# A two-layer attention trunk: half-row score products widened to 128 rows, latent scores in three split products, two residual column groups kept in DRAM

## The chip, the core and the metric

The kernel runs on one core of one Trainium2 chip. The metric is the device time of one execution in microseconds, the median of several runs; lower is better. The core's engines are named as in the profile: PE (TensorE, matrix products), PEld (its weight loads), DVE (VectorE), ACT (ScalarE), POOL (GpSimd) and SP (SyncE, which here issues every DMA).

## What is computed

The input x is 512 frames of 2048 channels, float32. Each of two layers does the following.

```
proj = rmsnorm(x) @ w_in           # 2048 -> dq, dk, dv (1024 each), cq 512, ckv 256, kr 64, gate 2048
# (A) differential attention, 8 heads, two softmax maps of width 64 per head
s = q @ k.T * scale + bias[:, m];  p = softmax(mask(s1)) - lam * softmax(mask(s2));  o_a = rmsnorm(p @ v)
# (B) latent attention, 8 heads: q and k/v come from the normalized latents cq and ckv
s = (qn @ kn.T + qr @ kr.T) * scale    # 128 plain channels per head and 64 rotary ones
o_b = softmax(mask(s)) @ v
x = x + (concat(o_a, o_b) * silu(gate)) @ w_out
```

A frame reads its own chunk of 64 frames and all earlier ones, so a block of 128 queries reads 128, 256, 384 or 512 keys. A last RMSNorm closes the trunk.

## The kernel before

**Split products.** A float32 operand is written as a high part (rounded to `fp32r`) and a low part (the rest). One product is then three products: high by high, high by low, low by high. `mm3` issues such a trio; nearly all of PE's work is trios of line 249 over projection weights. Products of plain float32 operands stand in the trace as two records each (`sc<-qkm`, line 523: 64 in the program, 128 in the trace).

**Weights.** Weights stream through a ring of units (2 or 4 blocks of 128 rows, 1024 columns in all). SP loads a unit to one of two `raw` buffers, ACT makes the high part (`whi`, line 195), DVE the low part (`wlo`, line 196), into four buffers each; when a unit is split, the load of the unit after the next one is issued (`pump`, `emit_dma`). The split runs up to two units ahead of PE. One unit is some 24 products of 512 columns.

**Order.** The program's order is written out by hand. A stage is a list of projection pieces for PE; `mix` spreads attention steps of the stage before between them. In a differential stage `i` the pieces project gates, values and queries/keys of two heads, and the steps are those of the two heads of stage `i-1`: `diff_scores` (step a), transposes of the probabilities (b), the product with v (c). In the latent part, stages `j` project two heads each (`mla_proj`) and a quarter of the output projection (`OD`, `j`), with the steps of `j-1` between them.

**Scores.** For 64-wide heads one product holds both parts of q: rows `half(m)` hold q's high part and the other 64 rows its low part, and k's high part stands in both halves. That gives high by high and low by high in one product over 128 rows (line 492). High by low is a second product that uses the 64 rows of `half(m)` alone (line 493):

```
nc.tensor.matmul(dst, lhsT=q[:, m], rhs=khi, start=first, stop=False)
nc.tensor.matmul(dst, lhsT=q[half(m), m], rhs=klo[half(m)], start=False, stop=True)
```

`diff_scores` does this for two maps (four products); `mla_scores` does a plain float32 product of the 128 unrotated channels (line 523) and then this pair for the rotary ones. There are 64 score steps of each kind in the program: 16 heads (8 per layer) by four widths.

**Buffers.** `big` has 16 pages of 8 KB per partition, which the residual `xs` (four column groups of 512), normalized activations, q/k pairs, gates and latents share. `evac_acc(c)` adds the first half of the output projection to `xs[c]`, `evac_om(c)` the second half, once all latent heads are done. `xs[c]` is loaded by `load_xc(c)` and stays in its page until then.

Of the kernel before, what the change touches and what calls it, by code (L numbers as in the profile page):

```python
# [14 lines left out]
ALU = mybir.AluOpType  # L15
# [39 lines left out]
def tile_hybrid_trunk(ctx, tc, x, norm_g, w_in, diff_lambda, diff_subln_g, mla_q_norm_g,  # L55
# [19 lines left out]
    bip = pool("bias", 2)  # L75
    tp = pool("tmp", 4)
    op = pool("o", 2)
    stp = pool("st", 16)
    keep = pool("keep", 4)
    krp = pool("kr", 1)  # L80
    klp = pool("kl", 3)
    pj = pool("pj", 4, bass.MemoryType.PSUM)
    at = pool("at", 4, bass.MemoryType.PSUM)
    dr = pool("dr", 1, bass.MemoryType.DRAM)
# [232 lines left out]
    with tc.manual_schedule():  # L317
# [12 lines left out]
        for q in range(4):  # L330
            load_x(x, 0, q)

        gsrc = const.tile([46, P], F32, name="gsrc")
        sp.dma_start(out=gsrc[0:32], in_=norm_g.rearrange("l (k p) -> (l k) p", p=P))
        sp.dma_start(out=gsrc[32:40], in_=mla_q_norm_g.rearrange("l (k p) -> (l k) p", p=P))
        sp.dma_start(out=gsrc[40:44], in_=mla_kv_norm_g.rearrange("l (k p) -> (l k) p", p=P))
# [5 lines left out]
        cosT = const.tile([P, NSB, ROPE], F32, name="cosT")  # L342
        sinT = const.tile([P, NSB, ROPE // 2], F32, name="sinT")
        dlam = B([P, DEPTH, 2, 2, DH], F32, "dlam")
        relb = const.tile([BUCKETS, MAPS], F32, name="relb")
        oneh = big.tile([BUCKETS, NVEC], F32, tag="B", name="oneh")
        def load_small():
            sp.dma_start(out=relb, in_=rel_bias)
            sp.dma_start(out=oneh, in_=onehot)
# [128 lines left out]
        def half(m):  # L478
            return slice(m * DH, (m + 1) * DH)
# [10 lines left out]
        def mm_stack(dst, q, khi, klo, m, first):  # L490

            nc.tensor.matmul(dst, lhsT=q[:, m], rhs=khi, start=first, stop=False)  # L492
            nc.tensor.matmul(dst, lhsT=q[half(m), m], rhs=klo[half(m)], start=False, stop=True)  # L493

        def diff_scores(l, hd, qb, bt, st_):
            w = (qb + 1) * P
            mx, sm = stat("mx"), stat("sum")
            s = []
            for m in range(2):
                bk = bank("sc")  # L500
                mm_stack(bk[:, :w], hd["qk"][:, 0, :, qb * P:(qb + 1) * P], hd["qk"][:, 1, m, :w], hd["kl"][:, :w], m, True)
                sm_t = T("s", smp, "sm")
                nc.vector.tensor_tensor_reduce(  # L503
                    out=sm_t[:, :w], in0=bk[:, :w], in1=bt[:, m, 512 - w:512], op0=ALU.add, op1=ALU.max,
                    scale=1.0, scalar=LOW, accum_out=mx[:, m:m + 1])
                s.append(sm_t)
            nc.vector.tensor_scalar(out=mx[:, 2:4], in0=mx[:, 0:2], scalar1=-1.0, scalar2=None, op0=ALU.mult)  # L507
            for m in range(2):
                nc.scalar.activation(s[m][:, :w], s[m][:, :w], AF.Exp, bias=mx[:, 2 + m:3 + m], accum_out=sm[:, m:m + 1])  # L509
            nc.vector.reciprocal(sm[:, 2:4], sm[:, 0:2])  # L510
            nc.vector.scalar_tensor_tensor(out=sm[:, 4:5], in0=sm[:, 3:4], scalar=neglam[:, l:l + 1], in1=sm[:, 0:1],
                                           op0=ALU.mult, op1=ALU.mult)
            nc.vector.scalar_tensor_tensor(out=s[0][:, :w], in0=s[1][:, :w], scalar=sm[:, 4:5], in1=s[0][:, :w],
                                           op0=ALU.mult, op1=ALU.add)
            st_["p"], st_["rc"] = s[0], sm[:, 2:3]

        def mla_scores(qk, par, j, rope, qb, st_):
            w = (qb + 1) * P
            scale = QH ** -0.5
            mx, sm = stat("mx"), stat("sum")  # L520
            bk = bank("sc")
            q = slice(qb * P, (qb + 1) * P)
            nc.tensor.matmul(bk[:, :w], lhsT=qk[:, par, q], rhs=qk[:, 2 + par, :w], start=True, stop=False)  # L523
            mm_stack(bk[:, :w], rope["q", j // 2][:, j % 2, :, q], rope["k"][:, 0, :w], rope["k"][:, 1, :w], par, False)
            nc.vector.memset(bk[0:CHUNK, w - CHUNK:w], NEG)
            nc.vector.tensor_reduce(out=mx[:, 0:1], in_=bk[:, :w], op=ALU.max, axis=AX.X)
            nc.vector.tensor_scalar(out=mx[:, 1:2], in0=mx[:, 0:1], scalar1=-scale, scalar2=None, op0=ALU.mult)  # L527
            s = T("s", smp, "sm")
            nc.scalar.activation(s[:, :w], bk[:, :w], AF.Exp, bias=mx[:, 1:2], scale=scale, accum_out=sm[:, 0:1])  # L529
            nc.vector.reciprocal(sm[:, 1:2], sm[:, 0:1])  # L530
            nc.vector.tensor_scalar(out=s[:, :w], in0=s[:, :w], scalar1=sm[:, 1:2], scalar2=None, op0=ALU.mult)
            st_["p"] = s
# [65 lines left out]
        def mla_items(l, j, qk, v, gate, rope):  # L598
            slots = []
            for hp in range(2):  # L600
                h = 2 * j + hp
                o_ = {}
                for qb in range(NSB):
                    st_ = {}

                    def a(hp=hp, qb=qb, st_=st_):
                        mla_scores(qk["t"], hp, j, rope, qb, st_)
                        if hp == 1 and qb == NSB - 1:
                            qk.pop("t")
                            if j % 2:  # L610
                                rope.pop(("q", j // 2))

                    def b(qb=qb, st_=st_):
                        transpose_p(qb, st_)

                    def c(hp=hp, qb=qb, o_=o_, st_=st_):
                        if qb == 0:
                            o_["bk"] = bank("oT")
                        for kb in range(qb + 1):
                            nc.tensor.matmul(o_["bk"][:, qb * P:(qb + 1) * P], lhsT=v["t"][:, kb, hp * P:(hp + 1) * P],  # L620
                                             rhs=st_["pt"][:, kb * P:(kb + 1) * P], start=kb == 0, stop=kb == qb)

                    slot = [a, b, c]
                    if qb == NSB - 1:
                        def d(h=h, o_=o_):
                            y = gate(h)
                            nc.vector.tensor_tensor(y, o_.pop("bk"), y, op=ALU.mult)

                        slot.append(d)
                    slots.append(slot)  # L630
            return pipeline(slots, MLAG)
# [5 lines left out]


        x1 = dr.tile([S, D], F32, name="x1")
        boundary = []  # L640
        for l in range(DEPTH):
            g = plan[l]
# [87 lines left out]
            for i in range(4):  # L730
                qk, v = {}, {}

                def evac_qk(b, bk, qk=qk):
                    if b < 2:
                        qk[b] = {"qk": B([P, 2, 2, S], F32R, "qk")}
                        split_stack(bk, qk[b]["qk"][:, 0], DH ** -0.5)
                        return
                    hd = qk[b - 2]
                    hd["kl"] = klp.tile([P, S], F32R, tag="kl", name="kl")
                    k = hd["qk"][:, 1]  # L740
                    for m in range(2):
                        acopy(k[half(m), m], bk[half(m)])
                    for m in range(2):
                        acopy(k[half(1 - m), m], bk[half(m)])
                        nc.vector.tensor_tensor(hd["kl"][half(m)], bk[half(m)], k[half(m), m].bitcast(F32), op=ALU.subtract)

                def evac_v(b, bk, v=v):
                    if "t" not in v:
                        v["t"] = vp.tile([P, NSB, 256], F32, tag="v", name="v")
                    (nc.vector.tensor_copy if b % 2 else acopy)(v["t"][:, b, :], bk[:, :256])  # L750

                pieces = []
                if i:
                    pieces += group(g["G", i - 1], 2, mm_T(ah), evac_gate(2 * i - 2))
                pieces += group(g["V", i], NSB, mm_S(ah, 256), evac_v, cost=2)
                pieces += group(g["QK", i], 4, mm_T(ah), evac_qk)
                mix(pieces, pend, MIX_DIFF)
                pend = diff_items(l, i, qk, v, gate_y)
# [22 lines left out]
            def load_xc(c, src=x if l == 0 else x1):  # L781
                for sb in range(NSB):
                    load_x(src, sb, c)

            load_xc(0)

            def act_y(y):
# [2 lines left out]
            def evac_acc(c):  # L790
                def evac(b, bk):
                    a = xs[c][:, b, :]
                    nc.vector.tensor_tensor(a, bk, a, op=ALU.add)
                return evac


# [97 lines left out]
            mix(group(g["QR"], NSB, mm_S(act_cq, 512), evac_qr), [])  # L894

            def mla_proj(j, qk, v):
                def evac_qn(b, bk):
                    if "t" not in qk:
                        qk["t"] = B([P, 4, S], F32, "qkm")
                    (nc.vector.tensor_copy if b % 2 else acopy)(qk["t"][:, b, :], bk)  # L900

                def mm_kv(bk, b, hi, lo, k, kb, first, last):
                    c = slice(b * 256, b * 256 + NOPE)
                    mm3(bk, (hi[:, k, c], lo[:, k, c]), act_kv(kb), True, first, last)

                def evac_kn(b, bk):
                    (nc.vector.tensor_copy if b % 2 else acopy)(qk["t"][:, 2 + b, :], bk)

                pieces = group(g["QN", j], 2, mm_T(act_cq), evac_qn)
                (u, _, _), = g["KV", j]  # L910
# [36 lines left out]
            for j in range(1, 4):  # L947
                pieces = mla_proj(j, *qkv[j]) + out_pieces(("OD", j), yd, evac_acc(j))
                if j == 3:
                    load_xc(3)  # L950
                    mix(pieces[:16], pend, MIX_MLA[2])
                    tail = pieces[16:]
                elif j == 2:
                    mix(pieces[:-8], pend, MIX_MLA[1])
                    load_xc(2)
# [114 lines left out]
```

## Time and profile before

| | |
|---|---|
| median of 3 runs | 1834.45 us (1833.92 to 1834.63) |
| profiled execution | 1835.62 us, span 1833.8 us |
| PE, PEld busy | 1804.4 us (98%), 1492.3 us (81%) |
| DVE, ACT, POOL busy | 952.9 us (52%), 710.1 us (39%), 32.2 us (2%) |
| DMA | 179.34 MB, 98 GB/s over the span |
| mean granted clock of TensorE | 0.997 |

The span is from the first to the last instruction of the profiled execution; its own time, 1835.62 us, also has what lies around it. PE's busy time counts a product until its modelled end, and products overlap in the pipeline: how long a product holds the engine is read from one start to the next.

### The profile page before, as it was taken

How to read it: one execution, taken by the hardware profiler on the slowest of the kernel's cores; microseconds unless marked ns; L12 is line 12 of the kernel's file. 1: busy time of each engine (PE TensorE's matmuls, PEld its weight loads, DVE VectorE, ACT ScalarE, POOL GpSimd, SP SyncE). 2: the span in 40 equal slices, each digit the busy share in tenths (PEclk: the TensorE clock that was granted, in tenths of full speed). 3: DMA queues.
4: the chain of work that ended last, by engine and by line, in shares of the span. 5: the costliest groups of instructions: out<-in, count | busy, mean ns of one | idle time of the engine just before them, and what ended most of it. 6: DMA issues, size and time to landing. Idle time of an engine off the chain costs nothing.

```text
span 1833.8 us, 23481 instructions
## 1 busy us (share of the span) xinstructions
PE 1804.4 (98%) x9245; PEld 1492.3 (81%) x9245; DVE 952.9 (52%) x1753; ACT 710.1 (39%) x1424; POOL 32.2 (2%) x53
## 2 busy tenths in 40 slices
PE   6999999999999999999999999999999999999997
PEld 4888888887878987878879887888887798878786
DVE  5426445453646774454362353644545667645554
ACT  5324444443443442333352343444443344433333
POOL 1000000000000000000000000000000000000000
PEclk9999999999999999999999999999999999999999
DMA  5543232232322431313333232323223224213223
GB/s 173 173 144 98 72 101 81 71 114 70 115 81 78 118 104 58 115 58 103 127 105 102 71 114 71 114 71 102 81 70 115 80 81 149 70 58 113 71 92 126
DMA packets 142330, 179.34 MB, mean 98 GB/s; under 512 B 16942, under 2 KB 94812, under 8 KB 142092
## 3 DMA queue, kind: packets, MB, share of 16 engines
q1 hardware_dynamic: 142220, 177.85, 31.7%
q8 instruction: 72, 1.18, 0.3%
q14 instruction: 38, 0.31, 0.1%
HBM read 169.39 MB, written 13.67 MB: 100 GB/s over the span
## 4 chain that ended last, share of the span: by engine, by line
PE 97%; ACT 1%; DVE 1%; issue 0%; DMA 0%; POOL 0%; SPq 0%; ACTq 0%; POOLq 0%; DVEq 0%
PE pj L249 81%; PE sc L493 4%; PE sc L492 2%; PE pT L309 2%; PE sc L523 2%; PE oT L620 2%; PE ov L573 2%; PE nT L309 1%; PE oT L309 0%; ACT xn L99 0%; PE cT L309 0%; ACT whi L195 0%; DMA xs<-in_x 0%; DVE nt L457 0%; POOL rs L314 0%
## 5 line engine op out<-in xcount | busy, mean ns | idle before, releaser
L196 DVE TENSOR_TENSOR wlo<-raw,whi 128x1024 fp32r<-128x1024 f32 (+1 forms) x272 | 327.7, 1211 | 323.9 <-ACT whi L195 316.5
L249 PE MATMUL pj<-hThi,whi 128*128 128x512 f32 x1024 | 413.6, 404 | 0.0
L249 PE MATMUL pj<-hThi,wlo 128*128 128x512 f32 x1024 | 400.0, 391 | 0.0
L249 PE MATMUL pj<-hTlo,whi 128*128 128x512 f32 x1024 | 399.5, 390 | 0.0
L195 ACT ACTIVATE whi<-raw 128x1024 fp32r<-128x1024 f32 (+1 forms) x272 | 282.6, 1047 | 180.6 <-PE pj L249 106.3
L249 PE MATMUL pj<-whi,yhl 128*128 128x512 f32 x1024 | 326.8, 400 | 0.0
L249 PE MATMUL pj<-whi,hThi 128*128 128x256 f32 (+2 forms) x768 | 243.1, 317 | 2.1 <-ACT hThi L99 2.1
L249 PE MATMUL pj<-whi,hTlo 128*128 128x256 f32 (+2 forms) x768 | 236.2, 308 | 0.0
L249 PE MATMUL pj<-wlo,hThi 128*128 128x256 f32 (+2 forms) x768 | 236.0, 307 | 0.0
L249 PEld LDWEIGHTS pj<-hThi,whi 128*128 128x128 f32 x1024 | 192.5, 188 | 43.3 <-issue 4.3
L249 PEld LDWEIGHTS pj<-hThi,wlo 128*128 128x128 f32 x1024 | 192.2, 188 | 41.4
L249 PEld LDWEIGHTS pj<-hTlo,whi 128*128 128x128 f32 x1024 | 192.8, 188 | 35.1
L249 PEld LDWEIGHTS pj<-whi,yhl 128*128 128x128 f32 x1024 | 184.3, 188 | 38.6 <-issue 3.5
L249 PE MATMUL pj<-wlo,yhl 128*128 128x512 f32 x512 | 200.5, 392 | 0.0
L509 ACT ACTIVATE s<-s,mx 128x128 f32<-128x128 f32 (+3 forms) x128 | 71.1, 557 | 294.0 <-DVE mx L507 294.0
L249 PEld LDWEIGHTS pj<-whi,hThi 128*128 128x128 f32 x768 | 147.2, 192 | 10.5 <-ACT hThi L99 2.5
L249 PEld LDWEIGHTS pj<-whi,hTlo 128*128 128x128 f32 x768 | 147.3, 192 | 5.5 <-DVE hTlo L462 0.7
L249 PEld LDWEIGHTS pj<-wlo,hThi 128*128 128x128 f32 x768 | 147.0, 191 | 5.6
L720 DVE RECIPROCAL ge<-ge 128x256 f32<-128x256 f32 x64 | 112.2, 1753 | 2.2
L249 PEld LDWEIGHTS pj<-wlo,yhl 128*128 128x128 f32 x512 | 96.1, 188 | 20.9
L503 DVE CUSTOM_DVE_ANT_0 s<-sc,bt 128x128 f32<-128x128 f32 (+3 forms) x128 | 59.7, 486 | 100.3 <-POOL bt L413 56.2
L529 ACT ACTIVATE s<-sc,mx 128x128 f32<-128x128 f32 (+1 forms) x64 | 33.8, 529 | 156.5 <-DVE mx L527 156.5
(153 smaller groups left out, 1876.1 us busy)
## 6 DMA issues: line engine op xcount, KB each, us to landing
raw<-in_w_in SPq DMA_DIRECT2D x112, 512.0 KB, 3.8
raw<-in_w_in SPq DMA_DIRECT2D x128, 256.0 KB, 2.9
raw<-in_w_out SPq DMA_DIRECT2D x64, 512.0 KB, 3.7
xs<-in_x SPq DMA_DIRECT2D x32, 256.0 KB, 5.3
bt<-btab SPq DMA_DIRECT2D x16, 512.0 KB, 5.4
btab<-vecd SPq DMA_DIRECT2D x16, 320.0 KB, 6.6
raw<-in_w_in SPq DMA_DIRECT2D x10, 480.0 KB, 3.7
raw<-in_mla_w_q_b SPq DMA_DIRECT2D x16, 256.0 KB, 3.2
```

Of the source, the lines that this page charges most:

```text
L195: nc.scalar.activation(hi[:, :n], raw[:, :n], AF.Copy)
L196: nc.vector.tensor_tensor(lo[:, :n], raw[:, :n], hi[:, :n].bitcast(F32), op=ALU.subtract)
L249: nc.tensor.matmul(dst, lhsT=a, rhs=b, start=first and t == 0, stop=last and t == 2)
L309: nc.tensor.transpose(dst, src, ident)
L492: nc.tensor.matmul(dst, lhsT=q[:, m], rhs=khi, start=first, stop=False)
L493: nc.tensor.matmul(dst, lhsT=q[half(m), m], rhs=klo[half(m)], start=False, stop=True)
L503: nc.vector.tensor_tensor_reduce(out=sm_t[:, :w], in0=bk[:, :w], in1=bt[:, m, 512 - w:512], op0=ALU.add, op1=ALU.max, scale=1.0, scalar=LO ...
L509: nc.scalar.activation(s[m][:, :w], s[m][:, :w], AF.Exp, bias=mx[:, 2 + m:3 + m], accum_out=sm[:, m:m + 1])
L523: nc.tensor.matmul(bk[:, :w], lhsT=qk[:, par, q], rhs=qk[:, 2 + par, :w], start=True, stop=False)
L573: nc.tensor.matmul(bk[:, :P], lhsT=st_["pt"][:, kb * P:(kb + 1) * P], rhs=v["t"][:, kb, hp * P:(hp + 1) * P], start=kb == 0, stop=kb == qb)
L620: nc.tensor.matmul(o_["bk"][:, qb * P:(qb + 1) * P], lhsT=v["t"][:, kb, hp * P:(hp + 1) * P], rhs=st_["pt"][:, kb * P:(kb + 1) * P], start ...
L720: nc.vector.reciprocal(e[:, c], e[:, c])
```

## The change

The low-part product of a score uses all 128 rows: `klo` gets one copy per map `m`, with k's low part in both halves, so that both halves of q meet it (this adds low by low). The `kl` buffers are twice as large, and there are two in place of three. The latent scores' plain float32 product becomes a trio of `fp32r` products, for which `mla_proj` keeps a high and a low part of q and k: the page `qkm` of a stage becomes two, and its evacuations become a copy on ACT and a subtraction on DVE each. To make room, `xs[0]` and `xs[1]` are stored to DRAM (`xa`) after the first half of the output projection and loaded again in stage `j == 3`. `stp` shrinks from 16 to 14 small buffers, and two small startup tiles share others' space.

```
-    stp = pool("st", 16)
+    stp = pool("st", 14)
-    klp = pool("kl", 3)
+    klp = pool("kl", 2)
...
-        gsrc = const.tile([46, P], F32, name="gsrc")
+        gsrc = T("gsrc")[:46, :P]
...
-            nc.tensor.matmul(dst, lhsT=q[half(m), m], rhs=klo[half(m)], start=False, stop=True)
+            nc.tensor.matmul(dst, lhsT=q[:, m], rhs=klo, start=False, stop=True)
...
-            nc.tensor.matmul(bk[:, :w], lhsT=qk[:, par, q], rhs=qk[:, 2 + par, :w], start=True, stop=False)
+            mm3(bk[:, :w], (qk["q"][:, par, 0, q], qk["q"][:, par, 1, q]),
+                (qk["k"][:, par, 0, :w], qk["k"][:, par, 1, :w]), True, True, False)
...
-                    hd["kl"] = klp.tile([P, S], F32R, tag="kl", name="kl")
+                    hd["kl"] = klp.tile([P, 2, S], F32R, tag="kl", name="kl")
...
-                        nc.vector.tensor_tensor(hd["kl"][half(m)], bk[half(m)], k[half(m), m].bitcast(F32), op=ALU.subtract)
+                        for n in (m, 1 - m):
+                            nc.vector.tensor_tensor(hd["kl"][half(n), m], bk[half(m)], k[half(m), m].bitcast(F32), op=ALU.subtract)
...
+            def park_xc(c):
+                sp.dma_start(out=xa[:, c * 512:(c + 1) * 512].rearrange("(b p) c -> p b c", p=P), in_=xs.pop(c))
...
+                    if c < 2 and b == NSB - 1:
+                        park_xc(c)
...
+                def evac_split(key, b, bk):
+                    if key not in qk:
+                        qk[key] = B([P, 2, 2, S], F32R, "qkm")
+                    hi = qk[key][:, b, 0]
+                    acopy(hi, bk)
+                    nc.vector.tensor_tensor(qk[key][:, b, 1], bk, hi.bitcast(F32), op=ALU.subtract)
...
-                    (nc.vector.tensor_copy if b % 2 else acopy)(qk["t"][:, b, :], bk)
+                    evac_split("q", b, bk)
...
-                    (nc.vector.tensor_copy if b % 2 else acopy)(qk["t"][:, 2 + b, :], bk)
+                    evac_split("k", b, bk)
...
                 if j == 3:
...
                     tail = pieces[16:]
+                    for c in range(2):
+                        load_xc(c, xa)
```

PE, at two steps of the first latent heads (`sc` is the score bank, `qkm` the unrotated q and k, `cqhi`/`cqlo` the latents, `krT`/`qrT` the rotary k and q); a row shows the size of the output, so line 493's rows (64 before, 128 after) read alike:

```order
 L249 MATMUL pj<-cqlo,whi 128x512
 L249 MATMUL pj<-cqhi,wlo 128x512
-L523 MATMUL sc<-qkm 128x256
+L249 MATMUL sc<-qkm 128x256 x3
 L492 MATMUL sc<-krT,qrT 128x256
 L493 MATMUL sc<-krT,qrT 128x256
-L523 MATMUL sc<-qkm 128x384
+L249 MATMUL sc<-qkm 128x384 x3
 L492 MATMUL sc<-krT,qrT 128x384
 L493 MATMUL sc<-krT,qrT 128x384
```

One product becomes three in its place; nothing else moves on PE.

DVE, at the end of the first differential stage, where the keys of two heads are evacuated (`kl` is k's low part) ahead of the next weight splits (`wlo`) and of the first score step (line 503):

```order
 L486 SCALAR_TENSOR_TENSOR qk<-pj,qk 64x512 x4
-L745 TENSOR_TENSOR kl<-pj,qk 64x512 x4
+L748 TENSOR_TENSOR kl<-pj,qk 64x512 x8
 L196 TENSOR_TENSOR wlo<-raw,whi 128x1024 x2
 L503 ISA s,mx<-sc,bt 128x128
```

Four more subtractions stand in the queue ahead of the two weight splits.

SP, in the last latent stage of layer 1, where the parked groups come back (`raw` are weight units, `x_147`/`x_148` the residual that layer 0 left, `fg` the final norm's gains):

```order
 L182 DMA raw<-in_w_out 128x2x512 x2
-L328 DMA xs<-x_148 128x512 x4
+L328 DMA xs<-x_147 128x512 x4
 L182 DMA raw<-in_w_out 128x2x512 x4
-L964 DMA fg<-in_final_norm_g 128x2048
+L328 DMA xs<-xa 128x512 x8
+L979 DMA fg<-in_final_norm_g 128x2048
 L182 DMA raw<-in_w_out 128x2x512 x14
```

Eight loads of 256 KB now stand between the loads of weight units; layer 0 has the same eight, without `fg` behind them.

## Rows read from the trace of the kernel before

**Rows 1.** The page: span, and busy time of each engine.
```profile
span 1833.8 us, 23481 instructions
PE 1804.4 (98%) x9245; PEld 1492.3 (81%) x9245; DVE 952.9 (52%) x1753; ACT 710.1 (39%) x1424; POOL 32.2 (2%) x53
```
**Rows 2.** The page: the chain that ended last, by engine and by line.
```profile
PE 97%; ACT 1%; DVE 1%; issue 0%; DMA 0%; POOL 0%; SPq 0%; ACTq 0%; POOLq 0%; DVEq 0%
PE pj L249 81%; PE sc L493 4%; PE sc L492 2%; PE pT L309 2%; PE sc L523 2%; PE oT L620 2%; PE ov L573 2%; PE nT L309 1%; PE oT L309 0%; ACT xn L99 0%; PE cT L309 0%; ACT whi L195 0%; DMA xs<-in_x 0%; DVE nt L457 0%; POOL rs L314 0%
```
**Rows 3.** Timeline of PE, a 128-wide differential step: start, duration, engine, instruction.
```profile
154.53 0.22 PE L492 MATMUL sc<-qk 128*128 128x128 f32 x1
154.68 0.32 PE L493 MATMUL sc<-kl,qk 64*128 64x128 f32 x1
154.93 0.33 PE L492 MATMUL sc<-qk 128*128 128x128 f32 x1
155.19 0.32 PE L493 MATMUL sc<-kl,qk 64*128 64x128 f32 x1
155.44 0.50 PE L249 MATMUL pj<-hThi,whi 128*128 128x512 f32 x1
155.78 0.40 PE L249 MATMUL pj<-hTlo,whi 128*128 128x512 f32 x1
156.01 0.39 PE L249 MATMUL pj<-hThi,wlo 128*128 128x512 f32 x1
...
158.06 0.39 PE L249 MATMUL pj<-hThi,wlo 128*128 128x512 f32 x1
```
**Rows 4.** Timeline of PE, a stretch of 256-wide projection products.
```profile
97.58 0.28 PE L249 MATMUL pj<-whi,hThi 128*128 128x256 f32 x1
...
98.78 0.28 PE L249 MATMUL pj<-whi,hTlo 128*128 128x256 f32 x1
```
**Rows 5.** Timeline of PE, a 512-wide differential step, followed by 256-wide products.
```profile
178.38 0.39 PE L492 MATMUL sc<-qk 128*128 128x512 f32 x1
...
179.97 0.38 PE L249 MATMUL pj<-whi,hThi 128*128 128x256 f32 x1
180.20 0.28 PE L249 MATMUL pj<-whi,hTlo 128*128 128x256 f32 x1
```
**Rows 6.** Timeline of PE, a 128-wide latent step.
```profile
672.92 0.38 PE L523 MATMUL sc<-qkm 128*128 128x128 f32 x2
...
673.55 0.50 PE L249 MATMUL pj<-cqhi,whi 128*128 128x512 f32 x1
673.89 0.39 PE L249 MATMUL pj<-cqlo,whi 128*128 128x512 f32 x1
```
**Rows 7.** Timeline of PE, a 512-wide latent step, followed by 256-wide products.
```profile
683.15 1.02 PE L523 MATMUL sc<-qkm 128*128 128x512 f32 x2
...
684.75 0.50 PE L249 MATMUL pj<-whi,ckvhl 128*128 128x256 f32 x2
685.09 0.28 PE L249 MATMUL pj<-wlo,ckvhl 128*128 128x256 f32 x1
```
**Rows 8.** Groups of weight loads: busy, mean ns, idle before and its releaser.
```profile
L493 PEld LDWEIGHTS sc<-kl,qk 64*128 64x128 f32 x128 | 23.4, 183 | 25.9 <-issue 22.2
```
**Rows 9.** Group on DVE by form: busy, mean ns, idle before.
```profile
L745 DVE TENSOR_TENSOR kl<-pj,qk 64x512 fp32r<-64x512 f32 x32 | 22.0, 689 | 19.1 <-ACT qk L99 19.1
```
**Rows 10.** Timeline of DVE ahead of the first differential scores.
```profile
149.79 2.36 DVE L196 TENSOR_TENSOR wlo<-raw,whi 128x1024 fp32r<-128x1024 f32 x2 [0.25 <-ACT whi L195]
```
**Rows 11.** DMA issues: count, KB of each, median us to landing.
```profile
raw<-in_w_out SPq DMA_DIRECT2D x64, 512.0 KB, 3.7
xs<-in_x SPq DMA_DIRECT2D x32, 256.0 KB, 5.3
fg<-in_final_norm_g SPq DMA_DIRECT2D x1, 1024.0 KB, 6.6
```
**Rows 12.** Windows, the first latent stage: length, then busy us by engine.
```profile
660.00:680.00 20.00, 20.00 (x107) 16.42 (x106) 15.88 (x31) 10.07 (x18) 0.00 (x0) 1.00 0.25 79
```

More of the change, by code (lines that the diff above doesn't have):

```diff
@@ L344, in tile_hybrid_trunk @@
         dlam = B([P, DEPTH, 2, 2, DH], F32, "dlam")
-        relb = const.tile([BUCKETS, MAPS], F32, name="relb")
-        oneh = big.tile([BUCKETS, NVEC], F32, tag="B", name="oneh")
+        relo = big.tile([BUCKETS, NVEC + MAPS], F32, tag="B", name="oneh")
+        oneh, relb = relo[:, :NVEC], relo[:, NVEC:]
         def load_small():
@@ L500, in diff_scores @@
                 bk = bank("sc")
-                mm_stack(bk[:, :w], hd["qk"][:, 0, :, qb * P:(qb + 1) * P], hd["qk"][:, 1, m, :w], hd["kl"][:, :w], m, True)
+                mm_stack(bk[:, :w], hd["qk"][:, 0, :, qb * P:(qb + 1) * P], hd["qk"][:, 1, m, :w], hd["kl"][:, m, :w], m, True)
                 sm_t = T("s", smp, "sm")
@@ L606, in a @@
                     def a(hp=hp, qb=qb, st_=st_):
-                        mla_scores(qk["t"], hp, j, rope, qb, st_)
+                        mla_scores(qk, hp, j, rope, qb, st_)
                         if hp == 1 and qb == NSB - 1:
-                            qk.pop("t")
+                            qk.clear()
                             if j % 2:
@@ L639, in tile_hybrid_trunk @@
         x1 = dr.tile([S, D], F32, name="x1")
+        xa = dr.tile([S, 2 * 512], F32, name="xa")
         boundary = []
@@ L896, in mla_proj @@
             def mla_proj(j, qk, v):
+                def evac_split(key, b, bk):
[4 more added lines that the diff above has]
+                    nc.vector.tensor_tensor(qk[key][:, b, 1], bk, hi.bitcast(F32), op=ALU.subtract)
                 def evac_qn(b, bk):
-                    if "t" not in qk:
-                        qk["t"] = B([P, 4, S], F32, "qkm")
-                    (nc.vector.tensor_copy if b % 2 else acopy)(qk["t"][:, b, :], bk)
+                    evac_split("q", b, bk)
                 def mm_kv(bk, b, hi, lo, k, kb, first, last):
```

## Prediction, on record before the result

> **What bounds the kernel now.** I read the page first. PE is busy for 1804.4 of the span's 1833.8 us, DVE for 952.9 and ACT for 710.1 [rows 1]. A busy PE alone could be a PE that is slow for some other reason, so I went to the chain that ended last: 97% of it is PE, 81% of it trios of line 249, and lines 492, 493 and 523, the score products, have 8% between them [rows 2]. Nothing else holds this kernel for long, so what counts is how long PE needs per product, and that is read from start to start, not from the durations. In a dense stretch nine products of 512 columns take 158.06 - 156.01 = 2.05 us, 0.228 each [rows 3]; ten of 256 columns take 1.20 us, 0.120 each [rows 4]. That is 0.054 us per 128 columns and 0.012 beside it; a 384-wide product takes 0.174 by it. At both widths the weight load that each product needs lies hidden behind the one before.
>
> Then I looked at a score step in the same way. Four products of 128 columns begin at 154.53, and the projection product behind them at 155.44: 0.91 us for products that stream 4 x 0.054 = 0.21 us of columns [rows 3]. The starts after the first are some 0.25 us apart, whether a full or a half-row product comes next: each change of shape, to 64 rows and back, seems to let the engine run empty and then to load weights in the open. The projection product behind the step shows the last part of it: its successor starts 0.34 us later in place of 0.228, so 0.11 us is one weight load that nothing hides. The loads of line 493 account for 25.9 us of idle weight path in the differential part alone, most of it with no releaser [rows 8]: no semaphore is waited for.
>
> **The change, part by part.** With all products at 128 rows I take the dense rate for the scores.
>
> *A differential step now.* From its first product to the product behind it, plus what that one loses: 0.91 + 0.11 = 1.02 us at 128 columns [rows 3]; (179.97 - 178.38) + (0.23 - 0.12) = 1.70 us at 512 [rows 5]. On the line between, 1.25 at 256 and 1.47 at 384. The sum over the widths is 5.44 us, and 16 heads give 87.0 us.
>
> *The same step after.* Four products, at 0.120, 0.174 and 0.228 us for 256, 384 and 512 columns. At 128 columns the trace has no dense `fp32r` product. Its columns would take 0.066 us, but a load in the open takes 0.11 and only one product lies ahead to hide it: bounds 0.066 and 0.11, and I take 0.11, since the load is measured and 0.066 would need it to be shorter. The widths sum to 0.632 us, four products to 2.53, 16 heads to 40.4 us. Gain: 46.6 us.
>
> *A latent step now*, with the float32 product's two passes: 0.63 + 0.11 = 0.74 us at 128 columns [rows 6], and (684.75 - 683.15) + (0.34 - 2 x 0.12) = 1.70 us at 512 [rows 7]; 1.06 and 1.38 between. The sum is 4.88 us, 16 heads 78.1 us. *After*: five products, 5 x 0.632 x 16 = 50.6 us. Gain: 27.5 us.
>
> Together 74.1 us. Both edits change PE's work alone by this; what they cost elsewhere I put at about 1 us of small waits, for these reasons.
>
> *Larger `kl`.* 32 more subtractions at 0.689 us, 22 us of DVE [rows 9], eight per stage. They fall in one burst: per stage 4 x 0.689 = 2.8 us stand ahead of the next two weight splits, with ACT's copies waiting in between, since the two engines read the same bank in turn. Those splits end at 152.15, the first of them half way, at about 151.0 [rows 10]; PE takes that unit's low part at 156.01 [rows 3]. The cover is 5 us for a delay of 2.8. If it were gone, each of the eight stages would lose up to 2.8 us, 22 us together.
>
> *Split `qkm`.* 32 subtractions for 16 copies on DVE, 16 more copies on ACT: about 11 us of DVE and 10 of ACT, in a stage where DVE is busy for 15.88 us of 20 at its worst [rows 12]. The evacuations release projection banks later by one subtraction, 0.69 us, while a group of two banks keeps PE for 24 products or 5.5 us.
>
> *Parking.* Per layer two stores of 1 MB and eight loads of 256 KB, all in SP's queue. Each store waits for DVE's last addition to its group, and the weight loads behind it wait too. But those loads need a `raw` buffer that a later split frees, and units for two splits ahead are issued before, so the wait falls where SP idles anyway. The loads wait for the last query product of stage 3, which lies before the pieces that issue them, so they start at once; they are wanted only when the second half of the output projection ends a group, over five units later. What can be late is the weight unit behind them. Four loads land in 5.3 us, so 2 MB may take twice that, 10.6, and the unit 3.7 more [rows 11]; it has two units of PE, 11 us, from its own issue, which comes a unit, 5.5 us, behind theirs. So 10.6 - 5.5 + 3.7 = 8.8 us against 11: I take nothing in layer 0, a little in layer 1, where `fg` adds 6.6 us [rows 11].
>
> *Smaller pools* are worth nothing: no buffer of `stp` outlives a few steps, and a head's last score lies a quarter of a stage before its `kl` is overwritten.
>
> **The sum.** The profiled execution's 1835.62 us, less 74.1, plus 1, is 1762.5 us; the runs' median lies 1.2 us below that execution, so 1761.5.
>
> **The rivals.**
>
> *The weight units come late* (slower than forecast). ACT works its list in order, so a split that waits for a load holds up the probabilities behind it. If 2 MB takes 2 x 6.6 = 13.2 us and `fg` is in front too, the next unit lands at 13.2 + 6.6 - 5.5 + 3.7 = 18 us against 11 in layer 1, and at 11.4 in layer 0; doubled for what queues behind, some 15 us: 1777. For it: 3 MB in one go is more than any stretch had. Against: a late split has a unit of cover left on PE.
>
> *Loads are not hidden between score products.* Then every score product of the new chain costs 0.108 us more at 256 columns and above and 0.064 at 128: 144 products per width, 144 x (0.064 + 3 x 0.108) = 56 us of the gain gone, 1817 us. Against it stand the dense rows, where loads at the same full rows hide [rows 3, 4]; for it, only that score products are few and change banks. The Trainium skill, TensorE: Matmul & The Clock Gate, section "Part 3: Packing small matmuls", says that a weight load overlaps with products in flight only when it goes to other row groups. By that the full-row loads could never hide, and the sum would be this rival's. The trace does not agree: 0.228 us per 512-wide product leaves no room for an open load of 0.11 beside 0.214 us of columns.
>
> *The gap is not the shape's.* If the second product of a pair is slow for another reason, differential steps gain nothing, and only the float32 product does: at 512 it costs 1.70 - 1.70/2 = 0.85 us against three at 0.228, at 128 0.74 - 0.51 = 0.23 against 0.33; over the widths 0.26 us, times 16, 4 us: 1830. Against it: trios add into one bank without any gap.
>
> *Slower than before.* Two `kl` buffers could make DVE wait for an old head's last score, with every weight split queued behind. To pass 1834 this has to take 73 us, 12 at each of the six boundaries between differential stages (three per layer). The last score step has 28 of the 38 shares of the steps ahead of it, so it would have to slip by a quarter of a stage.
>
> **Numbers.** The forecast, 1761.5, has 0.78 of the chance, from 1755 (128-wide products at 0.066 us: 144 x 0.044 = 6 us less) to 1768 (half the open cost of a late unit); late units 0.10, 1777; loads in the open 0.05, 1817; another reason for the gap 0.04, 1830; slower 0.03. The range is 1755 to 1775, which leaves out the last three and the far end of the second. A change within 0.2%, 3.7 us, is about what a measurement of this kernel can't tell from none; of the fourth case half is within it. Faster 0.94, same 0.03, slower 0.03.
>
> **What would show it.** Right: no product with 64 rows but small ones at startup; scores at 0.11 to 0.228 us from start to start; a differential step of 128 columns 0.44 us long and one of 512 0.91; the product behind a step without its 0.11; PE still 97% of the chain, the span near 1761. Wrong: weight loads of lines 249 and 493 in score steps with idle time of their own; waits of ACT's `whi` for `raw` in stage 3, or of PE for `wlo` after a stage's keys; 128-wide products at 0.16 us or more.

## The result, and the profile after

| | us, median (lowest to highest) | ratio to before, 95% interval |
|---|---|---|
| before, run beside it | 1834.54 (1833.92 to 1835.42) | |
| changed kernel | 1766.77 (1765.97 to 1767.97) | 0.9631 [0.9614, 0.9647] |
| forecast | 1761.5 (range 1755 to 1775) | 0.960 |

The change saves 67.8 us, where 73.1 were forecast: it lands inside the range and 5.3 us above the forecast. The profiled execution took 1767.97 us, 1.2 above the median, with a span of 1766.2.

The page of the changed kernel answers to [rows 1] and [rows 2]; first the span and the busy time of each engine, then the chain that ended last, by engine and by line.

```profile
span 1766.2 us, 23702 instructions
PE 1733.1 (98%) x9309; PEld 1493.5 (85%) x9309; DVE 980.4 (56%) x1801; ACT 710.5 (40%) x1440; POOL 32.0 (2%) x53
...
PE 93%; DVE 3%; ACT 2%; issue 1%; DMA 1%; POOL 0%; SPq 0%; ACTq 0%; POOLq 0%; DVEq 0%
PE pj L249 81%; PE ov L574 2%; PE pT L309 2%; PE oT L621 2%; PE sc L493 2%; PE sc L492 1%; PE sc L249 1%; PE nT L309 1%; DMA xs<-in_x 0%; DVE mx L527 0%; DVE wlo L196 0%; ACT whi L195 0%; DVE qkm L910 0%; PE oT L309 0%; DMA bt<-btab 0%
```

PE has 64 product records more (a trio counts three where a float32 product counted two) and is busy for 71 us less. The score products shrink from 8% of the chain to 4%. The unexpected part is that PE holds 93% of the chain and not 97%: DVE now has 3%, and among its lines stand `mx` (L527, the row maximum of a latent step's scores) and `qkm` (L910, the new subtraction). Both will turn up again.

The timeline of PE in the changed kernel shows whether the steps came out as worked out. The columns are start, duration, engine and instruction. First the 128-wide differential step of [rows 3]:

```profile
154.46 0.22 PE L492 MATMUL sc<-qk 128*128 128x128 f32 x1
154.52 0.28 PE L493 MATMUL sc<-kl,qk 128*128 128x128 f32 x1
154.63 0.27 PE L492 MATMUL sc<-qk 128*128 128x128 f32 x1
154.75 0.27 PE L493 MATMUL sc<-kl,qk 128*128 128x128 f32 x1
154.86 0.45 PE L249 MATMUL pj<-hThi,whi 128*128 128x512 f32 x1
155.14 0.39 PE L249 MATMUL pj<-hTlo,whi 128*128 128x512 f32 x1
```

Read from start to start, the products are 0.11 to 0.12 us apart behind the first. The step takes 154.86 - 154.46 = 0.40 us, and the product behind it loses 0.05 beside the dense 0.228, so the step costs 0.45 us where 0.44 was forecast and 1.02 stood before. In the step 128-wide products follow each other at 0.11 us, the upper of the prediction's two bounds (a weight load in the open), and not at 0.066 (their columns).

The same view of the 512-wide differential step of [rows 5]:

```profile
176.28 0.40 PE L492 MATMUL sc<-qk 128*128 128x512 f32 x1
...
177.21 0.28 PE L249 MATMUL pj<-whi,hThi 128*128 128x256 f32 x1
177.33 0.28 PE L249 MATMUL pj<-whi,hTlo 128*128 128x256 f32 x1
```

0.93 us for four products against a forecast of 0.91, and the product behind them is followed after 0.12 us, without the 0.11 that it lost before. And the 512-wide latent step of [rows 7], whose first row is the three products of high and low parts:

```profile
659.08 0.86 PE L249 MATMUL sc<-qkm 128*128 128x512 f32 x3
...
660.24 0.40 PE L249 MATMUL pj<-whi,ckvhl 128*128 128x256 f32 x2
```

Five products in 1.16 us, 5 x 0.228 = 1.14 forecast. The groups of weight loads say the same in one line, which answers to [rows 8]: the idle time ahead of line 493's loads went from 25.9 us to 2.8.

```profile
L493 PEld LDWEIGHTS sc<-kl,qk 128*128 128x128 f32 x128 | 24.2, 189 | 2.8
```

So the products did what was forecast, to about 0.02 us per step, and most of the 5.3 us is not in them. It stands in the waits of PE in the changed kernel (what waits, for what: us in total, times, longest us):

```profile
...
PE pT L309 <- ACT s L530: 3.4, 4, 0.9
...
PE pT L309 <- DVE s L513: 0.4, 1, 0.4
```

The rows left out, for `nT`, `gbk` and `pj`, PE had before too, nearly as long, but none for `pT`. In the latent stages PE now waits four times, twice in each layer, ahead of the transposes of a step's probabilities (`pT`), for an exponential of ACT (`s`, L530). The timeline of all engines around the second of these waits shows what ACT is late for; a bracket is the idle time before the instruction and what ended it.

```profile
747.97 0.34 PE L493 MATMUL sc<-krT,qrT 128*128 128x384 f32 x1
...
748.41 0.69 DVE L910 TENSOR_TENSOR qkm<-pj,qkm 128x512 fp32r<-128x512 f32 x1
...
750.03 0.58 ACT L530 ACTIVATE s<-sc,mx 128x384 f32<-128x384 f32 x1 [1.65 <-DVE mx L528]
...
750.76 1.06 ACT L195 ACTIVATE whi<-raw 128x1024 fp32r<-128x1024 f32 x1
...
750.93 0.42 DVE L532 TENSOR_SCALAR s<-s,sum 128x384 f32<-128x384 f32 x1
...
751.85 1.23 DVE L196 TENSOR_TENSOR wlo<-raw,whi 128x1024 fp32r<-128x1024 f32 x1 [0.50 <-ACT whi L195]
...
752.16 0.38 PE L309 MATMUL pT<-ident,s 128*128 128x128 f32 x2
...
752.99 0.68 DVE L910 TENSOR_TENSOR qkm<-pj,qkm 128x512 fp32r<-128x512 f32 x1
753.68 0.11 DVE L526 MEMSET sc<- 64x64 f32 x1
753.83 0.69 DVE L527 TENSOR_REDUCE mx<-sc 128x1 f32<-128x512 f32 x1
754.42 0.28 PE L493 MATMUL sc<-krT,qrT 128*128 128x128 f32 x1
...
754.74 0.69 ACT L530 ACTIVATE s<-sc,mx 128x512 f32<-128x512 f32 x1 [2.43 <-DVE mx L528]
755.57 0.55 PE L309 MATMUL pT<-ident,s 128*128 128x128 f32 x3 [0.87 <-ACT s L530]
...
755.89 0.38 ACT L99 ACTIVATE pt<-pT 128x256 f32<-128x256 f32 x1
```

To be read from the bottom: PE waits 0.87 us for an exponential that waited for DVE's row maximum. Ahead of that maximum's mask and reduction (L526, L527) stands a `qkm` subtraction, 0.68 us, and it can't start before the weight split of L196. That split waited for ACT's copy, the copy for the exponential before it, and that one for a row maximum that had a `qkm` subtraction ahead of it too, at 748.41. So two subtractions lie one behind the other in one chain, 1.37 us.

The three transposes do not need the probabilities of that exponential: they turn over those of the step with 384 columns, which DVE had scaled by 751.35 (L532). What they lack is a place to write to. In the program the scores, the transposes and the outputs of the attention steps share four banks (`bank`). At 755.4 one holds the head's output, one the scores that PE has just made (754.42), one the two transposes of 752.16, which ACT copies out only at 755.89, and the fourth the scores that the late exponential is still reading. That it is the bank is read from the program and the times together; no run has a fifth one.

At the same place of the kernel before, the mask and the reduction followed the split directly, and the transposes followed the last score product, of half rows there, after 0.25 us:

```profile
780.65 1.23 DVE L196 TENSOR_TENSOR wlo<-raw,whi 128x1024 fp32r<-128x1024 f32 x1 [0.49 <-ACT whi L195]
...
781.88 0.11 DVE L525 MEMSET sc<- 64x64 f32 x1
...
784.66 0.33 PE L493 MATMUL sc<-krT,qrT 64*128 64x128 f32 x1
...
784.91 0.55 PE L309 MATMUL pT<-ident,s 128*128 128x128 f32 x3
```

DVE's share tells nothing of it. The window around this wait in the changed kernel (length, then busy us of PE, PEld, DVE, ACT and POOL):

```profile
745.00:765.00 20.00, 19.13 (x116) 16.90 (x115) 13.61 (x41) 9.49 (x25) 0.00 (x0) 1.00 0.17 54
```

PE loses 0.87 of 20 us in a window in which DVE is idle for 6.4.

### The profile page after: what moved, and what is told of

Its sections match the earlier page's. It is cut to its first block, busy times and chain, and to the rows that moved or that the text cites. A ratio compares the mean times of both kernels' runs of the same rounds, so it can differ in the third digit from the quotient of the medians.

```text
span 1766.2 us, 23702 instructions
## 1 busy us (share of the span) xinstructions
PE 1733.1 (98%) x9309; PEld 1493.5 (85%) x9309; DVE 980.4 (56%) x1801; ACT 710.5 (40%) x1440; POOL 32.0 (2%) x53
## 4 chain that ended last, share of the span: by engine, by line
PE 93%; DVE 3%; ACT 2%; issue 1%; DMA 1%; POOL 0%; SPq 0%; ACTq 0%; POOLq 0%; DVEq 0%
PE pj L249 81%; PE ov L574 2%; PE pT L309 2%; PE oT L621 2%; PE sc L493 2%; PE sc L492 1%; PE sc L249 1%; PE nT L309 1%; DMA xs<-in_x 0%; DVE mx L527 0%; DVE wlo L196 0%; ACT whi L195 0%; DVE qkm L910 0%; PE oT L309 0%; DMA bt<-btab 0%
## 5 line engine op out<-in xcount | busy, mean ns | idle before, releaser
L196 DVE TENSOR_TENSOR wlo<-raw,whi 128x1024 fp32r<-128x1024 f32 (+1 forms) x272 | 327.5, 1211 | 297.6 <-ACT whi L195 290.4
L530 ACT ACTIVATE s<-sc,mx 128x128 f32<-128x128 f32 (+1 forms) x64 | 33.8, 528 | 133.9 <-DVE mx L528 133.9
```

Of the source, the lines that this page charges most:

```text
L196: nc.vector.tensor_tensor(lo[:, :n], raw[:, :n], hi[:, :n].bitcast(F32), op=ALU.subtract)
```

## Experiments

Two rounds of four kernels, each round on one chip beside the kernel before (1834.82 us in the first, 1834.99 in the second, medians of 15 runs).

| kernel | us, median (lowest to highest) | ratio to before, 95% interval |
|---|---|---|
| differential half alone | 1789.73 (1789.44 to 1790.62) | 0.9755 [0.9742, 0.9768] |
| full rows alone, latent product in float32 | 1766.77 (1766.00 to 1766.92) | 0.9628 [0.9615, 0.9641] |
| half-row products in pairs | 1802.56 (1800.27 to 1802.92) | 0.9822 [0.9808, 0.9835] |
| larger `kl` alone | 1835.95 (1834.82 to 1836.44) | 1.0006 [0.9997, 1.0015] |
| the change again | 1767.74 (1765.21 to 1768.55) | 0.9631 [0.9618, 0.9644] |
| subtractions put off | 1762.37 (1761.26 to 1763.28) | 0.9605 [0.9592, 0.9618] |
| subtractions left out | 1763.68 (1762.39 to 1764.04) | 0.9611 [0.9598, 0.9625] |
| parking alone | 1834.68 (1833.84 to 1835.73) | 0.9999 [0.9990, 1.0008] |

**The differential half alone.** The changed kernel with its latent steps, evacuations and residual as before.

```
-            nc.tensor.matmul(dst, lhsT=q[:, m], rhs=klo, start=False, stop=True)
+            nc.tensor.matmul(dst, lhsT=q[rows, m], rhs=klo[rows], start=False, stop=True)
...
+            nc.tensor.matmul(bk[:, :w], lhsT=qk["t"][:, par, q], rhs=qk["t"][:, 2 + par, :w], start=True, stop=False)
+            mm_stack(bk[:, :w], rope["q", j // 2][:, j % 2, :, q], rope["k"][:, 0, :w], rope["k"][:, 1, :w], par, False, half(par))
```

> The widened low-part product in the differential steps alone; latent steps (plain float32 product, half-row rotary product) and residual pages as before the change. Theory S (each change of shape costs PE an empty array and a weight load in the open): the differential term alone, 1834.5 - 46.6 = 1788 us (1785 to 1791), differential steps of 0.44, 0.48, 0.70, 0.91 us, latent steps still 0.74 to 1.70. Rival G (the second product of a pair is slow for another reason): 1834.

1789.73 us: 45.1 us saved, against 46.6 in the sum's first term. The rival on which the gap is not the shape's is out.

**Full rows alone.** The changed kernel with the rotary part of the latent scores at full rows, but the latent product itself in plain float32, `qkm` not split and nothing parked.

```
-            mm3(bk[:, :w], (qk["q"][:, par, 0, q], qk["q"][:, par, 1, q]),
-                (qk["k"][:, par, 0, :w], qk["k"][:, par, 1, :w]), True, True, False)
+            nc.tensor.matmul(bk[:, :w], lhsT=qk["t"][:, par, q], rhs=qk["t"][:, 2 + par, :w], start=True, stop=False)
```

> All low-part products over 128 rows, differential and rotary, but the latent product stays plain float32: no split of qkm, no parking. From the rows of before a latent step loses 0.28, 0.38, 0.40, 0.40 us by the rows alone, 16 heads 23.3 us, so theory S gives 1788 - 23.3 = 1764.6 us (1762 to 1768), and the trio is worth about 4 us at PE, which the waits of the changed kernel (4.1 us at four places ahead of latent transposes) eat: same time as the changed kernel. Rival F (the float32 product costs a change-over of its own, so the trio carries most of the latent gain): 1775 or more.

1766.77 us, the same median as the changed kernel to the hundredth. What this kernel lacks of the change, the three products, the split and the parking, brings no time in sum. PE has no wait for `pT` here. From the differential half alone to this one are 23.0 us: that is what full rows are worth in the latent steps. The timeline of PE in this kernel shows why so much of the latent term lies there, at the 512-wide latent step:

```profile
658.79 1.02 PE L523 MATMUL sc<-qkm 128*128 128x512 f32 x2
...
660.11 0.40 PE L249 MATMUL pj<-whi,ckvhl 128*128 128x256 f32 x2
```

The step takes 1.32 us with the float32 product in it and 1.16 with three products in its place; with the half-row product it took 1.70, with what the product behind it lost [rows 7].

**Half-row products in pairs.** The kernel before, with the order of a differential step's products changed and nothing else: first both full-row products, then both half-row ones, into two banks. The change of shape is made twice per step and not four times.

```
-                mm_stack(bk[:, :w], hd["qk"][:, 0, :, qb * P:(qb + 1) * P], hd["qk"][:, 1, m, :w], hd["kl"][:, :w], m, True)
+                nc.tensor.matmul(bks[m][:, :w], lhsT=q2[:, m], rhs=hd["qk"][:, 1, m, :w], start=True, stop=False)
+            for m in range(2):
+                nc.tensor.matmul(bks[m][:, :w], lhsT=q2[half(m), m], rhs=hd["kl"][half(m), :w], start=False, stop=True)
```

> The kernel before, with the four products of a differential step in another order: both full-row products first, then both half-row ones (rows 0 to 63, then 64 to 127). Same products, two changes of shape per step in place of four. Theory S: half of the excess of a step goes, 0.4 us, times 64 steps 25 us: 1809 us; if the two half-row products also overlap in time, 8 to 10 us more, 1800. Rival P (each half-row product costs its own price wherever it stands): 1834.

1802.56 us: 32.3 us saved, with no larger `kl` and no added work. The timeline of PE in this kernel, a 128-wide step and a 512-wide one:

```profile
154.96 0.33 PE L502 MATMUL sc<-qk 128*128 128x128 f32 x2
155.22 0.33 PE L504 MATMUL sc<-kl,qk 64*128 64x128 f32 x2
155.48 0.50 PE L249 MATMUL pj<-hThi,whi 128*128 128x512 f32 x1
155.81 0.39 PE L249 MATMUL pj<-hTlo,whi 128*128 128x512 f32 x1
...
177.41 0.63 PE L502 MATMUL sc<-qk 128*128 128x512 f32 x2
177.97 0.50 PE L504 MATMUL sc<-kl,qk 64*128 64x512 f32 x2
178.40 0.39 PE L249 MATMUL pj<-whi,hThi 128*128 128x256 f32 x1
178.62 0.28 PE L249 MATMUL pj<-whi,hTlo 128*128 128x256 f32 x1
```

The 128-wide step costs 0.52 us and 0.10 behind it, against 1.02 before. The two half-row products take 155.48 - 155.22 = 0.26 us until the next product starts, where one alone took 0.25 [rows 3]; at 512 columns the pair takes 178.40 - 177.97 = 0.43. The second costs nothing: the two records lie in one stretch of 0.33 and 0.50 us, as long as that of one alone (0.32 [rows 3] and 0.50), so they stream at the same time. The result lies between the 1809 and the 1800 that were expected without and with that, nearer to 1800.

The prices fit. Against full rows a step of the kernel before has (1.02 - 0.45) / 4 = 0.14 us of excess per change of shape at 128 columns and (1.70 - 0.93) / 4 = 0.19 at 512. Two changes, and a second half-row product that costs nothing, make 0.45 - 0.11 + 2 x 0.14 = 0.62 us and 0.93 - 0.23 + 2 x 0.19 = 1.08; the steps measure 0.62 and 1.09.

**Larger `kl` alone.** "Full rows alone" with the score products at half rows again; the 32 added subtractions stay. So it differs from the kernel before by them and the smaller pools.

```
-            nc.tensor.matmul(dst, lhsT=q[:, m], rhs=klo, start=False, stop=True)
+            nc.tensor.matmul(dst, lhsT=q[half(m), m], rhs=klo[half(m)], start=False, stop=True)
```

> The doubled low part of k is written (32 more subtractions, two buffers of twice the size, 14 small buffers), but the products still read the half rows; latent part and pages as before. The cost of that burst alone: by the cover of 5 us for 2.8 us of delay nothing, 1834.5 us (1834 to 1836). Rival: up to 2.8 us in each of eight stages, 1857.

1835.95 us, a ratio whose interval holds 1: at most 2.8 us, and perhaps nothing. Its group on DVE, which answers to [rows 9], has all 64 subtractions, 44.0 us in place of 22.0.

**The change again**, unchanged, as the mark for the second round.

> The changed kernel once more, beside the three that follow on the same chip: 1766.8 us (1765.5 to 1768), with four waits of about 1 us ahead of latent transposes.

1767.74 us, with the same wait of PE for L530 in its profile, 3.4 us in four times, and none for L513. Its spread, 3.3 us, is the widest of the eight.

**Subtractions put off.** The changed kernel; the same 32 `qkm` subtractions, but each is issued behind the next latent step's maximum and exponential (or ahead of the next evacuation or of the value pieces, if one comes first) and not at the evacuation.

```
+            flush_low()
...
+                    flush_low()
...
                     acopy(hi, bk)
-                    nc.vector.tensor_tensor(qk[key][:, b, 1], bk, hi.bitcast(F32), op=ALU.subtract)
+                    lows.append(lambda: nc.vector.tensor_tensor(lo, bk, hi.bitcast(F32), op=ALU.subtract))
```

> The changed kernel, with the subtraction that makes the low part of a latent q or k put off until the next score step has its maximum and its exponential issued. Theory Q (the four waits of about 1 us ahead of latent transposes come from these subtractions standing ahead of the softmax steps in DVE's queue): the waits go, 1766.8 - 4.1 = 1762.7 us (1762 to 1764.5). Rival T (there is simply less PE time between scores and transposes now): 1766.8, the waits stay.

1762.37 us: all of its runs lie below all of the change's. PE has 96% of the chain that ended last here, against 93% in the changed kernel. The waits of PE have no row for `pT`, and these are all that the view lists:

```profile
PE nT L309 <- ACT xn L99: 11.0, 9, 2.4
PE gbk L362 <- DMA gsrc<-in_mla_q_norm_g: 7.0, 1, 7.0
PE pj L249 <- ACT hThi L99: 2.1, 1, 2.1
```

Its timeline at the place where the chain of the changed kernel began, the step with 384 columns, and where PE waited there:

```profile
745.71 0.35 PE L493 MATMUL sc<-krT,qrT 128*128 128x384 f32 x1
...
746.95 0.68 DVE L918 TENSOR_TENSOR qkm<-pj,qkm 128x512 fp32r<-128x512 f32 x1
747.07 0.58 ACT L536 ACTIVATE s<-sc,mx 128x384 f32<-128x384 f32 x1 [1.26 <-DVE mx L534]
...
752.19 0.28 PE L493 MATMUL sc<-krT,qrT 128*128 128x128 f32 x1
752.30 0.52 PE L309 MATMUL pT<-ident,s 128*128 128x128 f32 x3
```

The subtraction runs beside the exponential, and PE goes from the last score product to the transposes in 0.11 us. The exponential starts 1.36 us after the step's last score product (745.71), against 2.06 in the changed kernel (747.97 to 750.03).

**Subtractions left out.** The changed kernel without the `qkm` subtractions; the products read the high part where the low part belongs, so three products run, on other numbers.

```
-            mm3(bk[:, :w], (qk["q"][:, par, 0, q], qk["q"][:, par, 1, q]),
...
+            mm3(bk[:, :w], (qk["q"][:, par, 0, q], qk["q"][:, par, 0, q]),
...
-                    nc.vector.tensor_tensor(qk[key][:, b, 1], bk, hi.bitcast(F32), op=ALU.subtract)
```

> The changed kernel without those subtractions: the high part is read where the low part belongs, so the computation is changed there. Same products on PE, 22 us less on DVE. Theory Q: the four waits go, 1762.7 us (1762 to 1764.5). Rival T: 1766.8, the waits stay.

1763.68 us, and no wait for `pT` either. That is 4.1 us below the change run beside it. PE's products are as many and as wide as in the changed kernel, so the time comes from the subtractions; that it is their place, and not the work, shows in the kernel that only puts them off. The rival, that there is simply less PE time between scores and transposes, falls in both kernels.

**Parking alone.** The kernel before with the two column groups stored and loaded as in the change.

```
+                    if c < 2 and b == NSB - 1:
+                        park_xc(c)
...
+                    for c in range(2):
+                        load_xc(c, xa)
```

> The kernel before, with the two residual groups stored to DRAM and loaded again as in the change, and nothing else. By the prediction nothing, 1834.5 us (1834 to 1836). Rival L (weight units come late behind the 2 MB of loads): 1837 to 1850, with waits of ACT for the weights in the last latent stage, above all of the second layer.

1834.68 us, no difference. The 2 MB of loads in the last latent stage delay nothing that ACT waits for: its longest waits for weights there are 4.7 and 4.2 us in the two layers, 4.8 and 4.2 before. What comes late is the unit behind the first store. In the first latent stage of this kernel (SPq is SP's queue of DMA issues):

```profile
647.08 0.37 SPq L787 DMA_DIRECT2D xa<-xs  x1
...
650.80 0.97 SPq L182 DMA_DIRECT2D raw<-in_mla_w_q_b  x2
...
657.38 1.06 ACT L195 ACTIVATE whi<-raw 128x1024 fp32r<-128x1024 f32 x1 [9.83 <-DMA raw<-in_mla_w_q_b]
```

and before:

```profile
652.63 1.06 ACT L195 ACTIVATE whi<-raw 128x1024 fp32r<-128x1024 f32 x1 [4.55 <-DMA raw<-in_mla_w_q_b]
```

The store waits in SP's queue for DVE's addition, and the loads behind it wait with it: ACT gets this unit 4.8 us later, and the one at the same place of the second layer waits for 10.2 us against 5.2. PE has no wait behind either.

## Why the prediction was right, and what was off

**The gap between score products is the change of shape: right, and shown.** Undoing it by full rows saves 45.1 us in the differential steps; changing shape twice and not four times per step, at the same half rows, saves 32.3. A half-row product with a price of its own, paid once for a pair, would give the second saving too. Against it stands the full-row product between two half-row ones, which holds PE for 0.26 us [rows 3] where 0.11 will do at full rows. Its weight load starts with it and not ahead of it, as the timeline of PEld in the kernel before shows:

```profile
154.93 0.19 PEld L492 LDWEIGHTS sc<-qk 128*128 128x128 f32 x1
```

In the dense stretch behind the step a load starts 0.23 us ahead of its product (155.78 for the product at 156.01). The trace agrees with the Trainium skill, TensorEngine Tiling (Array Packing), section "Key Properties", which says that a change of tiling mode drains the engine. It gives no price.

**The dense rate holds for score products: right.** 0.11 us at 128 columns, 0.23 at 512, loads hidden. The rival of loads in the open would have ended at 1817; here loads at the same full rows hide behind the products ahead. The Trainium skill, TensorE: Matmul & The Clock Gate, section "Part 3: Packing small matmuls — row/col tiling", says that a load overlaps only when its row group differs; in the same section it also names loads to a background weight buffer, which the prediction did not take up. The measurement decides against the first statement taken alone. Between the bounds 0.066 and 0.11 for 128 columns, the upper was right.

**The terms of the sum.** Differential steps: 46.6 us forecast, 45.1 measured; the 1.5 us are inside the interval of that ratio (plus or minus 2.4 us), and the larger `kl`'s possible 1.1 is in them. Latent steps: 27.5 forecast; from the differential half alone to the kernel with the subtractions put off it is 1789.73 - 1762.37 = 27.4 us, across two rounds whose kernels before differ by 0.2. Full rows make 23.0 of it, and the three products the other 4.4; the prediction did not state this split, though its rows give it (4.2 us in the working of the rival at 1830).

The traces give the same terms without the noise of the medians. Summed over the 64 steps of a kind, each from its first product to the product behind it with what that one loses, the differential steps go from 87.3 us to 41.1, a gain of 46.2 us; less the 1.1 that the larger `kl` may cost, that is the 45.1 measured. The latent steps go from 78.4 to 52.5 where the subtractions are put off or left out, a gain of 25.9; in the changed kernel, waits included, they take 56.6, and with full rows and the float32 product 55.4. So the latent term was 1.6 us too high, 0.025 per step, and the three products earn 2.9 us by this count.

**The step that failed: "about 1 us of small waits", in its part on the split `qkm`.** The prediction put the added 11 us of DVE against a stage in which DVE has room, and against the release of projection banks. It asked when the subtraction lets go of a projection bank, and not what is queued behind it on DVE: a latent step's mask, reduction and maximum, for which ACT's exponential waits; and until the exponential is done, PE's transposes have no free bank to write to. Each subtraction delays that by its 0.69 us, and where two of them lie in one chain the cover is gone: the transposes start 755.57 - 754.42 = 1.15 us after the product ahead of them where 0.11 will do (752.19 to 752.30 with the subtractions put off), so 1.04 us is lost, four times: 4.2 us in place of 1. The two kernels without these waits are 4.1 and 5.4 us faster than the change run beside them. So what the three products earned, 2.9 us by the steps and 4.4 by the medians, was given back in the same stages, and "full rows alone" and the changed kernel have the same time. The prediction's cover for the banks was also read too wide: 24 products fill two query banks, but a key bank is filled by six, 1.4 us. No wait of PE for a projection bank came of it.

**Costed at nothing, and not to be told from nothing:** parking (0.9999 [0.9990, 1.0008]) and the smaller pools with the larger `kl` (1.0006 [0.9997, 1.0015]). The rival of late weight units did not have its condition met: behind the parked loads no wait of ACT for weights grew. The working of the stores was wrong in part, since the wait behind the first store does not fall where SP idles anyway and doubles ACT's longest wait for a unit of `in_mla_w_q_b`; PE had split units in hand and lost nothing.

**The sum.** As written it gives 1835.62 - 74.1 + 1 - 1.2 = 1761.3, not 1761.5. Of the 5.3 us between forecast and median, some 3.1 are the waits beyond the 1 us allowed, and 2.0 are the two terms' steps (0.4 and 1.6).

**What stays open.** The kernels with the subtractions put off and left out differ by 1.3 us, with the same steps on PE and the same waits; their runs overlap, and runs of this spread can't tell whether that is real. The 1.6 us of the latent term lie in part in steps behind an `oT` product, whose first product at 512 columns holds PE for 0.31 us in place of 0.23; why is not shown. The wait of 0.4 us for DVE's `s` (L513) stands in this one profiled execution, and not in that of the change run again.

## What to carry to other kernels

A half-row product in a stream of full-row ones costs the changes of shape, not its rows: pad it to full rows, or, if there is no room for the padded operand, put the half-row products of different rows side by side, which kept 32 of 45 us here with no added work. When an edit adds work to an engine that is far from full, price it by what is queued behind it, who waits for that and what it holds meanwhile (here a bank of scores), and not by the engine's share; putting it behind the urgent work recovers the loss, and the version that does so here (1762.37 us) beats both kernels. When a change has several parts, run each alone: here full rows alone had all of the gain.

## What was not expected of the hardware

Two products of 64 rows, one on rows 0 to 63 and the other on rows 64 to 127, into different banks, take no longer than one: 0.26 us for two against 0.25 for one at 128 columns. At 512 columns a single half-row product of the kernel before, in a latent step, ran from 780.50 to the next product's start at 780.93, 0.43 us, and the pair takes 0.43 too. The Trainium skill, TensorE: Matmul & The Clock Gate, section "Part 3: Packing small matmuls — row/col tiling", says that products in different row groups run concurrently; the trace agrees, in this kernel alone, since no other run has two half-row products side by side.
